# Attention scores of a hybrid encoder layer: 288 contraction rows packed as 128 + 128 + 32, and operands of the recurrence split by how long they live

## The chip, the cores and the metric

One core of one Trainium2 chip runs the whole layer in one launch. The metric is device time in microseconds (us). The engines named below are TensorE (PE, with its weight loads listed as PEld), VectorE (DVE), ScalarE (ACT), GpSimd (POOL) and SyncE (SP), which only issues transfers. TensorE's granted clock has two levels, 1.2 and 2.4 GHz; the profile gives it as a share of the higher one.

## The reference, cut to what matters

The layer normalises x (2048 positions, 1024 channels), projects it once, mixes positions in three branches (a Fourier transform, a gated delta-rule recurrence in both directions, attention with six heads), gates and projects each branch, merges them, and projects once more. The change touches attention and the recurrence:

```
s = einsum('bqhd,bkhd->bhqk', qn, k_nope) + einsum('bqhd,bkd->bhqk', qr, k_rope)   # 64 + 32 rows
p = softmax(s * 96 ** -0.5)
o = einsum('bhqk,bkhd->bqhd', p, v)
S = S * w + (S a) b^T + v k^T ;  y = S r         # per head (6), per direction (2), 2048 steps
```

`k_rope` is the same for all heads. All values are float32.

## The kernel before, in words

Products that need float32 accuracy are done in three passes: an operand is split in two parts, hi and lo, that TensorE multiplies in one pass each (type fp32r), and `mm3` (L140 to 144) adds hi*hi, hi*lo and lo*hi in one accumulator. Products of plain float32 operands (values, transposes, the recurrence) are given as they are; TensorE runs a float32 matmul as two instructions.

**Phase 1** (up to about 1408 us of the span) projects x. Its last part is `columns` (L359): three attention gates end it, two of them with their four position blocks in turn (L371). Beside it run `units` (L540), which builds the recurrence's operands per 64-position chunk and stores them in the scratch tensors `X_d` and `V_d`, and `inverses` (L736), a long chain of small VectorE operations on a tile `M` that is read from `X_d` and written back to it.

**Phase 2** (`phase2`, L1195, about 1408 to 2262 us) is attention over 24 windows: a head pair and 256 queries. A window has four units of 128 queries and one head, 96 units in all. For unit n, TensorE's order is written out by hand: four times [the scores of unit n+2 for one block of 512 keys (`scores`, three passes over 96 rows), four transposes of unit n's probabilities (`probs`)]; after the second and the fourth, some pieces of the values of the window before (`values`), and one `step` of a background list. VectorE moves each score block from PSUM to `S` and takes its maximum (L1307, "eviction" below), ScalarE does one exponential per unit (L1314), and the transposed blocks are copied to `PT`, two by ScalarE (L1033) and two by VectorE (L1032). Scores have three PSUM buffers, transposes two, values one.

The background list is, one after the other: the end of `units`, 12 waiting steps (`wait2`), `recurrence` (32 chunks of three steps: `seq_r` with the outputs `seq_y` of the chunk before, `seq_u`, `seq_s`; each step is 24 to 72 small TensorE instructions and two VectorE operations that the next step needs), `rwkv_out` (eight blocks of VectorE, ScalarE and GpSimd work on the recurrence's output), and `phase3_early` (weights of the last phase). The recurrence takes the two PSUM banks that are left. When it is over, `merged` is set and all value pieces come after the fourth block.

`seq_load` (L963) reads a chunk's operands: per direction one tile part of 8*64 columns from `X_d`, and two from `V_d`. `window_open` (L1254) requests a window's queries, `window_load` (L1267) a head pair's keys (two tiles with one buffer each), and, once, the values of all heads.

**Phase 3** does the projections and the output.

The framework fixes the order on every engine but TensorE in this stretch by priorities and its own estimate of times, and puts in the waits.

Of the kernel before, what the change touches and what calls it, by code (L numbers as in the profile page):

```python
# [90 lines left out]
class Trunk:  # L91
    def __init__(self, tc, ins, out, stop=99):
# [39 lines left out]
        self.wait2 = 12  # L132
# [145 lines left out]
    def scratch(self):  # L278
# [15 lines left out]
        self.qn_d = t([6 * 64, T // QB, 2 * QB], F32, name="qn_d")  # L294
        self.qr_d = t([6 * 32, T // QB, 2 * QB], F32, name="qr_d")
        self.kn_d = t([6 * 64, T // QB, 2 * QB], F32, name="kn_d")
        self.kr_d = t([32, T // QB, 2 * QB], F32, name="kr_d")
# [61 lines left out]
    def columns(self):  # L359
# [8 lines left out]
        gates = [(O_ZCG + n * P, self.to_gate(self.gc_d[n], self.nc.gpsimd)) for n in range(3)]  # L368
# [326 lines left out]
    def unit_x(self, it, up):  # L695
        nc, w, rev, V3 = self.nc, it["win"], it["rev"], self.V3
        X = it["X"] = up.tile([P, UC, 8, C], F32, tag="X", name=f'X{it["nm"]}', bufs=self.xb)
        for h in range(2):
            eng = nc.vector if h == 0 else nc.gpsimd
            ps = slice(64 * h, 64 * h + 64)  # L700
            eng.tensor_tensor(rev(X[ps, :, 2 * h, :]), V3(w["kk"][ps]), it["gexc"][ps], ALU.mult)
            eng.tensor_tensor(rev(X[ps, :, 2 * h + 1, :]), V3(w["r"][ps]), it["ginc"][ps], ALU.mult)

    def unit_gram(self, it, gps):
        nc, w, d, X, BK = self.nc, it["win"], it["d"], it["X"], it["BK"]
        p, u, nm = w["p"], w["u"], it["nm"]
        mk = lambda m, hv: m[hv].unsqueeze(1).to_broadcast([64, UC, P])
# [5 lines left out]
        for q in range(UC):  # L713
            for h, ps in enumerate((lo, up_)):
                nc.tensor.matmul(g[h][:, q, :], BK[ps, q, :], X[ps, q, 2 * h:2 * h + 2, :], start=True, stop=True)
        for h in range(2):
            kr, br = (up_, lo) if h == 0 else (lo, up_)
            nc.vector.tensor_tensor(X[br, :, 4:6, :].rearrange("p c s t -> p c (s t)"),
                                    g[h][br], mk(self.msk, br), ALU.mult)
            nc.vector.tensor_tensor(X[kr, :, 2 * h:2 * h + 2, :].rearrange("p c s t -> p c (s t)"),  # L720
                                    g[h][kr], mk(self.msr if d else self.msk, kr), ALU.mult)
        nc.scalar.activation(X[:, :, 6:8, :].rearrange("p c s t -> p c (s t)"), tp, AF.Copy)
# [5 lines left out]
    def unit_bonus(self, w, up, gps):  # L728
# [4 lines left out]
        nc.vector.tensor_tensor(bv, bp[:, :UN], w["v"], ALU.mult)  # L733
        nc.sync.dma_start(self.bv_d[p][:, w["sl"]], bv)

    def inverses(self, ip):  # L736
# [5 lines left out]
        def lanes(p, k):  # L742
            d, h, c = k // 4, k // 2 % 2, k % 2 * 16
            return (M[16 * k:16 * k + 16],
                    self.X_d[d][c:c + 16, :, p, 4 * C:5 * C].rearrange("c (h s) t -> c h s t", h=2)[:, h])
# [64 lines left out]
    def rope_tables(self, rp):  # L810
# [33 lines left out]
        for s in range(2):  # L844
            o = rp.tile([P, 2, W], F32R, tag="ko", name=f"ko{s}", bufs=2)
            self.split(o[:, 0, :], o[:, 1, :], z[:, 1, s, :], nc.gpsimd)
            nc.sync.dma_start(self.kr_d[16 * s:16 * s + 16].rearrange("f b t -> b f t"),
                              o.rearrange("p a t -> p (a t)").bitcast(F32))
# [14 lines left out]
    def mla_window(self, u, W, mp, mps, ones, wqh, wql, wkh, wkl):  # L863
# [28 lines left out]
        def emit(ps, M, dst):  # L892
# [3 lines left out]
            nc.sync.dma_start(dst, o[:M].rearrange("p a t -> p (a t)").bitcast(F32))  # L896

        for j in range(3):
# [3 lines left out]
            emit(ps[:, :W], P, self.kn_d[j * P:(j + 1) * P, u, :])  # L902
# [9 lines left out]
        for j in range(3):  # L912
# [4 lines left out]
            emit(ps[:, :W], P, self.qn_d[j * P:(j + 1) * P, u, :])  # L917
# [10 lines left out]
        qd = self.qr_d[:, u, :].rearrange("(h s f) t -> s h f t", s=2, f=16)  # L928
        for s in range(2):
            emit(t[:96, s, :], 96, qd[s])  # L930
# [3 lines left out]
    def recurrence(self):  # L934
        tc, nc = self.tc, self.nc
        with tc.tile_pool(name="sq", bufs=1, side="right", reuse_waits="tile") as sp, \
# [10 lines left out]
            yield  # L947
# [15 lines left out]
    def seq_load(self, sp, n):  # L963
        nc = self.nc
        X = sp.tile([P, 2, NP, 8, C], F32, tag="X", name=f"sX_{n}", bufs=2)
        W = sp.tile([P, 2, NP, 4, C], F32, tag="W", name=f"sW_{n}", bufs=3)
        for d in range(2):
            c = n if d == 0 else NCH - 1 - n
            nc.sync.dma_start(X[:, d].rearrange("p n s t -> p n (s t)"), self.X_d[d][c])
# [3 lines left out]
        return X, W  # L973
# [6 lines left out]
    def seq_r(self, ps, pad, n, cur):  # L980
        R, (X, W) = ps[0], cur
        for p in range(NP):
            for d, h, hs in self.lanes():
                self.nc.tensor.matmul(R[hs, d, p, :], X[:, d, p, 2 * h, :], W[:, d, p, 2 * h + 1, :], start=True, stop=True)
# [4 lines left out]
    def seq_u(self, ps, pad, n, cur):  # L989
        nc, U, (X, W) = self.nc, ps[1], cur  # L990
        for p in range(NP):
            for d, h, hs in self.lanes():
                nc.tensor.matmul(U[hs, d, p, :], X[:, d, p, 4, :], pad[0][h][:, d, p, :], start=True, stop=True)
# [503 lines left out]
```

## Time and profile before

| | us |
|---|---|
| median of three runs | 2632.16 (2631.91 to 2633.26) |
| the profiled execution | 2634.32 |
| its span, first to last instruction | 2632.5 |
| TensorE matmul busy | 2504.7 (95% of the span) |
| VectorE / ScalarE / GpSimd busy | 1737.4 / 991.9 / 848.0 |

Matmuls overlap their own tail with the next one, so a busy TensorE can still be given more; what one costs is the distance from its start to the start of the next. All numbers are from one execution.

### The profile page before, as it was taken

How to read it: one execution, taken by the hardware profiler on the slowest of the kernel's cores; microseconds unless marked ns; L12 is line 12 of the kernel's file. 1: busy time of each engine (PE TensorE's matmuls, PEld its weight loads, DVE VectorE, ACT ScalarE, POOL GpSimd, SP SyncE). 2: the span in 40 equal slices, each digit the busy share in tenths (PEclk: the TensorE clock that was granted, in tenths of full speed). 3: DMA queues.
4: the chain of work that ended last, by engine and by line, in shares of the span. 5: the costliest groups of instructions: out<-in, count | busy, mean ns of one | idle time of the engine just before them, and what ended most of it. 6: DMA issues, size and time to landing. Idle time of an engine off the chain costs nothing.

```text
span 2632.5 us, 46308 instructions
## 1 busy us (share of the span) xinstructions
PE 2504.7 (95%) x17295; PEld 2040.8 (78%) x17295; DVE 1737.4 (66%) x3432; ACT 991.9 (38%) x1929; POOL 848.0 (32%) x1124
## 2 busy tenths in 40 slices
PE   7989999999999999989998899999998899999998
PEld 6778887877777777768776688878876677799997
DVE  6236564388888859579398567766767787544444
ACT  6354443355555521111113333333355565322221
POOL 2244433355555511212220233323322220334342
PEclk9999999999999999999998899999999999999999
DMA  4353434477777774552733655665544311645452
GB/s 167 95 146 121 149 125 157 141 262 256 245 262 247 246 156 128 130 145 86 136 84 111 157 169 186 192 186 166 174 149 125 101 53 59 194 128 154 131 154 78
DMA packets 318443, 404.86 MB, mean 154 GB/s; under 512 B 56078, under 2 KB 225097, under 8 KB 317130
## 3 DMA queue, kind: packets, MB, share of 16 engines
q1 hardware_dynamic: 310762, 382.99, 49.0%
q0 software_dynamic: 7456, 18.91, 3.0%
q8 instruction: 137, 2.24, 0.4%
q14 instruction: 88, 0.72, 0.1%
HBM read 236.91 MB, written 164.89 MB: 153 GB/s over the span
## 4 chain that ended last, share of the span: by engine, by line
PE 38%; DVE 13%; DMA 8%; issue 4%; POOL 1%; ACT 1%; SPq 1%; DVEq 0%; POOLq 0%; ACTq 0%
PE av L1334 5%; PE tp L1322 4%; DVE M L760 4%; DVE tmp L758 4%; PE sc L142 3%; PE sc L144 2%; PE sc L143 2%; PE po L144 2%; PE po L143 2%; PE po L142 2%; PE p L144 2%; PE p L143 2%; PE p L142 2%; DVE S L1307 1%; PE mm L142 1%
## 5 line engine op out<-in xcount | busy, mean ns | idle before, releaser
L142 PE MATMUL mm<-hh,wh 128*128 128x512 f32 x1536 | 613.8, 400 | 6.5 <-ACT z L483 3.2
L144 PE MATMUL mm<-hh,wl 128*128 128x512 f32 x1536 | 604.0, 394 | 2.8 <-POOL wl L419 2.6
L143 PE MATMUL mm<-hl,wh 128*128 128x512 f32 x1536 | 605.2, 394 | 0.0
L142 PEld LDWEIGHTS mm<-hh,wh 128*128 128x128 f32 x1536 | 291.7, 190 | 72.1 <-ACT z L483 5.2
L144 PEld LDWEIGHTS mm<-hh,wl 128*128 128x128 f32 x1536 | 291.6, 190 | 65.1 <-POOL wl L419 4.1
L143 PEld LDWEIGHTS mm<-hl,wh 128*128 128x128 f32 x1536 | 291.9, 190 | 58.2 <-issue 1.0
L1307 DVE TENSOR_SCALAR_CACHE_REDUCE S<-sc 128x512 f32<-128x512 f32 x384 | 260.7, 688 | 73.2 <-PE sc L144 67.5
L419 POOL TENSOR_TENSOR wl<-wr,wh 128x256 fp32r<-128x256 f32 x192 | 172.2, 910 | 419.1 <-ACT wh L418 406.2
L1322 PEld LDWEIGHTS tp<-c_id,S 128*128 128x128 f32 x1536 | 192.9, 143 | 84.9 <-ACT PT L1033 14.5
L1322 PE MATMUL tp<-c_id,S 128*128 128x128 f32 x1536 | 237.8, 278 | 21.0 <-ACT S L1314 8.6
L1314 ACT ACTIVATE S<-S,m 128x2048 f32<-128x2048 f32 x96 | 192.2, 2003 | 161.7 <-DVE m L1312 161.7
L758 DVE TENSOR_TENSOR tmp<-M 128x62 f32<-128x62 f32 (+30 forms) x186 | 171.7, 923 | 96.5 <-DMA zm_d<-z 41.3
L142 PE MATMUL sc<-K,Q 96*128 96x512 f32 x384 | 188.4, 491 | 19.7 <-DVE S L1307 13.8
L1033 ACT ACTIVATE PT<-tp 128x512 f32<-128x512 f32 x192 | 113.2, 591 | 225.8 <-PE tp L1322 222.7
L1334 PE MATMUL av<-PT,V 128*64 128x256 f32 x1536 | 180.0, 385 | 0.0
L760 DVE TENSOR_TENSOR M<-M,tmp 128x62 f32<-128x62 f32 (+30 forms) x186 | 170.7, 918 | 5.8
L418 ACT ACTIVATE wh<-wr 128x256 fp32r<-128x256 f32 x192 | 74.4, 412 | 238.7 <-DMA wr<-in_w_in_dram 149.2
L144 PE MATMUL sc<-K,Q 96*128 96x512 f32 x384 | 155.4, 405 | 0.0
L143 PE MATMUL sc<-K,Q 96*128 96x512 f32 x384 | 154.8, 403 | 0.0
L483 ACT ACTIVATE z<-mm 128x512 f32<-128x512 f32 (+1 forms) x120 | 70.3, 589 | 217.7 <-PE mm L144 107.2
L1334 PEld LDWEIGHTS av<-PT,V 128*64 128x64 f32 x1536 | 105.4, 137 | 57.8 <-issue 11.2
L1432 POOL TENSOR_TENSOR g<-g 128x256 f32<-128x256 f32 x128 | 98.8, 774 | 143.2 <-DVE g L1430 100.6
(388 smaller groups left out, 4945.4 us busy)
## 6 DMA issues: line engine op xcount, KB each, us to landing
X_d<-X SPq DMA_DIRECT2D x96, 512.0 KB
sX<-X_d SPq DMA_DIRECT2D x64, 768.0 KB
wr<-in_w_in_dram SPq DMA_DIRECT2D x193, 128.0 KB
zm_d<-z SPq DMA_DIRECT2D x96, 256.0 KB
g<-zm_d SPq DMA_DIRECT2D x64, 384.0 KB
uu<-u_d SPq DMA_DIRECT2D x24, 512.0 KB
ul<-lo_d SPq DMA_DIRECT2D x48, 256.0 KB
sW<-V_d SPq DMA_DIRECT2D x128, 96.0 KB
```

What stands on the lines that cost most here:

```text
L142: mm(out, lh, rh, start=start, stop=False)
L143: mm(out, lh, rl, start=False, stop=False)
L144: mm(out, ll, rh, start=False, stop=stop)
L419: nc.gpsimd.tensor_tensor(wl[:, ks, :], wr, wh[:, ks, :].bitcast(F32), ALU.subtract)
L758: nc.vector.tensor_tensor(tv, M[:, 0:j, j:j + 1].to_broadcast([P, j, n]), M[:, j:j + 1, j + 1:C].to_broadcast([P, j, n]), ALU.mult)
L760: nc.vector.tensor_tensor(M[:, 0:j, j + 1:C], M[:, 0:j, j + 1:C], tv, ALU.add)
L1033: return self.nc.scalar.activation(out, src, AF.Copy)
L1307: nc.vector.tensor_scalar(u["S"][:, ks], sc, 1.0, -3.4e38, ALU.mult, ALU.max, accum_out=u["m4"][:, kb:kb + 1])
L1314: nc.scalar.activation(S, S, AF.Exp, scale=SM_SCALE, bias=m4[:, 5:6], accum_out=u["win"]["rs"][:, col:col + 1])
L1322: nc.tensor.transpose(tp[:, k, :], u["S"][:, (4 * g + k) * P:(4 * g + k + 1) * P], self.ident)
L1334: nc.tensor.matmul(av[64 * h:64 * h + 64, 0:QB], self.V[:, k, (2 * hp + h) * 64:(2 * hp + h + 1) * 64], PT[k // 4][:, k % 4, h, :], start= ...
L1432: nc.gpsimd.tensor_tensor(g, g, acc, ALU.add)
```

## The change

The scores' 3 * 96 = 288 contraction rows are laid out anew: pass one is [q_nope hi, q_nope hi] against [k_nope hi, k_nope lo], pass two [q_nope lo, q_rope hi, q_rope hi] against [k_nope hi, k_rope hi, k_rope lo], both over 128 rows; q_rope lo against k_rope hi is left, 32 rows. For it `KC` holds k_rope hi with one block of 512 keys in each quarter of the partitions, and `QC` q_rope lo four times; `scores_rest` does the four blocks of a unit with four matmuls, each on its own 32 rows and into its own accumulator, ahead of the unit's other scores. Score and transpose tiles now share one pool of five PSUM buffers. Scratch layouts keep hi and lo apart. Values are loaded per head pair.

The chunk operands `X_d` are reordered: 0 to 4 are what `seq_r`, `seq_u` and `seq_s` read, 5 to 7 what `seq_y` reads a step later; `seq_load` reads `V_d` first, then the two parts into tiles of their own. `wait2` goes from 12 to 9, and `recurrence` waits two steps more after its first load. `rwkv_out` requests its blocks two ahead and on ScalarE's queue, and its first addition moves from VectorE to GpSimd. One VectorE product in `unit_bonus` becomes a ScalarE copy and a GpSimd product. After the recurrence VectorE copies one `PT` block of four instead of two. Two gates of `columns` go through the position blocks in pairs, and their stores are issued by ScalarE instead of GpSimd. Weights of phase 3 are split one step after they are requested.

```diff
-        self.wait2 = 12
+        self.wait2 = 9
-        for tb in range(NTB):
+        for tbs in ((0, 1), (2, 3)):
             for w, consume in cols:
-                self.project(w, P, tb, consume, True)
+                for tb in tbs:
+                    self.project(w, P, tb, consume, True)
...
+            g4 = g[h].rearrange("p c (s t) -> p c s t", s=2)
+            nc.vector.tensor_tensor(X[br, :, 2:8:5, :], g4[br], mk(self.msk, br), ALU.mult)
+            nc.vector.tensor_tensor(X[kr, :, h:h + 6:5, :], g4[kr], mk(self.msr if d else self.msk, kr), ALU.mult)
...
-        nc.vector.tensor_tensor(bv, bp[:, :UN], w["v"], ALU.mult)
+        nc.scalar.activation(bv, bp[:, :UN], AF.Copy)
+        nc.gpsimd.tensor_tensor(bv, bv, w["v"], ALU.mult)
...
+        X = sp.tile([P, 2, NP, 5, C], F32, tag="X", name=f"sX_{n}", bufs=2)
+        Z = sp.tile([P, 2, NP, 3, C], F32, tag="Z", name=f"sZ_{n}", bufs=2)
...
+            nc.sync.dma_start(X[:, d].rearrange("p n s t -> p n (s t)"), self.X_d[d][c][:, :, 0:5 * C])
...
+            nc.sync.dma_start(Z[:, d].rearrange("p n s t -> p n (s t)"), self.X_d[d][c][:, :, 5 * C:8 * C])
...
-                    nc.sync.dma_start(t, src[:, :, sl].rearrange("n p t -> p n t"))
+                    nc.scalar.dma_start(t, src[:, :, sl].rearrange("n p t -> p n t"))
...
-                tc.tile_pool(name="scps", bufs=self.scb, space=PSUM, reuse_waits="tile") as scps, \
-                tc.tile_pool(name="tpps", bufs=self.tpb, space=PSUM, reuse_waits="tile") as tpps, \
+                tc.tile_pool(name="scps", bufs=5, space=PSUM, reuse_waits="tile") as scps, \
...
+                self.KC = ap.tile([P, TB], F32R, name="KC")
+                nc.sync.dma_start(self.KC.bitcast(F32), self.kr_d[0].rearrange("p (k t) -> k p t", t=TB))
...
+        for h in range(2):
+            qn, qr = [[src[a, (2 * hp + h) * n:(2 * hp + h + 1) * n, sl] for a in range(2)]
+                      for src, n in ((self.qn_d, 64), (self.qr_d, 32))]
+            for dst, src, n in ((qf[:, 0, h], qn[0], 64), (qf[0:64, 1, h], qn[1], 64), (qf[64:P, 1, h], qr[0], 32), (cf[:, h], qr[1], 32)):
+                nc.sync.dma_start(dst, src.unsqueeze(0).to_broadcast([dst.shape[0] // n, n, QB]))
...
+    def scores_rest(self, u):
+        qs = slice(u["q"] * P, (u["q"] + 1) * P)
+        u["sc"] = [self.scps.tile([P, TB], F32, tag="s", name=f'sc{u["nm"]}{kb}') for kb in range(NTB)]
+        for kb, sc in enumerate(u["sc"]):
+            ps = slice(32 * kb, 32 * kb + 32)
+            self.nc.tensor.matmul(sc, u["win"]["QC"][ps, u["h"], qs], self.KC[ps], start=True, stop=False)
...
-        self.mm3(sc, Q[:, 0, qs], Q[:, 1, qs], K[:, ws, 0, :], K[:, ws, 1, :], True, True)
+        for n in range(2):
+            nc.tensor.matmul(sc, Q[:, n, u["h"], qs], K[:, n, ks], start=False, stop=n == 1)
...
-        tp = self.tpps.tile([P, 4, P], F32, tag="tp", name=f'tp{u["nm"]}{g}')
+        tp = self.scps.tile([P, 4, P], F32, tag="s", name=f'tp{u["nm"]}{g}')
...
-        self.copy(g in self.ptd, dst, tp)
+        self.copy(g in (self.ptd[1:] if self.merged else self.ptd), dst, tp)
```

## Rows read from the trace of the kernel before

**Rows 1.** Busy us of each engine, clock and DMA by stretch: the recurrence, then after it.
```profile
1471.00:1940.00 469.00, 462.52 (x6048) 374.99 (x6049) 321.49 (x821) 171.85 (x258) 140.41 (x202) 0.99 0.57 171
1940.00:2262.00 322.00, 291.36 (x1974) 218.40 (x1974) 236.95 (x585) 180.97 (x248) 55.82 (x42) 0.97 0.34 97
```

**Rows 2.** Waits of TensorE, 1470 to 1940: waiter, awaited, us in total, times, longest.
```profile
PE sps L984 <- DMA sW<-V_d: 10.2, 2, 7.4
...
PE tp L1322 <- DVE PT L1032: 0.3, 1, 0.3
```

**Rows 3.** Waits of TensorE, 1940 to 2265.
```profile
PE sc L142 <- DVE S L1307: 13.8, 5, 6.5
PE tp L1322 <- ACT PT L1033: 6.7, 8, 2.8
...
PE tp L1322 <- DVE PT L1032: 4.4, 8, 2.7
```

**Rows 4.** Timeline during the recurrence: start, us, engine, line, instruction, count.
```profile
1700.81 0.40 PE L143 MATMUL sc<-K,Q 96*128 96x512 f32 x1
...
1701.04 0.40 PE L144 MATMUL sc<-K,Q 96*128 96x512 f32 x1
...
1701.28 0.60 PE L1322 MATMUL tp<-c_id,S 128*128 128x128 f32 x4
...
1701.81 0.92 PE L1006 MATMUL sps<-sW,sX 128*64 128x64 f32 x24
...
1702.66 0.50 PE L142 MATMUL sc<-K,Q 96*128 96x512 f32 x1
...
1703.00 0.39 PE L143 MATMUL sc<-K,Q 96*128 96x512 f32 x1
```

**Rows 5.** Timeline of TensorE in phase 1, around matmuls over 64 rows.
```profile
702.26 0.60 PE L711 MATMUL tp<-c_id,BK 128*128 128x128 f32 x4
702.79 1.16 PE L715 MATMUL g<-X,BK 64*128 64x128 f32 x16
```

**Rows 6.** Groups of the whole span: count | busy us, mean ns | idle before.
```profile
L715 PE MATMUL g<-X,BK 64*128 64x128 f32 x768 | 55.8, 285 | 0.0
...
L711 PE MATMUL tp<-c_id,BK 128*128 128x128 f32 x192 | 28.7, 272 | 0.0
```

**Rows 7.** The same groups, VectorE and ScalarE, 1940 to 2265.
```profile
L1307 DVE TENSOR_SCALAR_CACHE_REDUCE S<-sc 128x512 f32<-128x512 f32 x153 | 103.4, 685 | 14.3 <-PE sc L144 13.8
L1032 DVE COPY PT<-tp 128x512 f32<-128x512 f32 x81 | 55.6, 686 | 13.6 <-PE av L1334 11.0 <-PE tp L1322 2.6
L1307 DVE DVE_READ_ACCUMULATOR S<-sc 128x1 f32 x153 | 12.7, 83 | 0.0
...
L1062 DVE TENSOR_TENSOR ry<-ry,ry 128x768 f32<-128x768 f32 x8 | 8.6, 1074 | 21.7 <-issue 11.2 <-DMA ry<-y_d 10.5
```

**Rows 8.** The same groups, ScalarE, 1940 to 2265.
```profile
L1314 ACT ACTIVATE S<-S,m 128x2048 f32<-128x2048 f32 x39 | 78.0, 1999 | 32.0 <-DVE m L1312 32.0
L1033 ACT ACTIVATE PT<-tp 128x512 f32<-128x512 f32 x81 | 47.5, 589 | 66.6 <-PE tp L1322 63.6 <-PE av L1334 2.9
```

**Rows 9.** The same groups, VectorE, 1470 to 1940.
```profile
L1307 DVE TENSOR_SCALAR_CACHE_REDUCE S<-sc 128x512 f32<-128x512 f32 x195 | 132.8, 691 | 51.1 <-PE sc L144 46.1
...
L996 DVE COPY sW<-sps 64x384 f32<-64x384 f32 x64 | 35.5, 554 | 21.6 <-PE sps L993 17.2 <-DMA sX<-X_d 3.0
```

**Rows 10.** Timeline of SP's queue where the recurrence begins.
```profile
1466.71 1.18 SPq L971 DMA_DIRECT2D sW<-V_d  x2
```

**Rows 11.** Timeline of TensorE there; in brackets its idle time and what ended it.
```profile
1471.57 0.84 PE L984 MATMUL sps<-sW,sX 128*64 128x64 f32 x4 [7.39 <-DMA sW<-V_d]
1475.24 1.65 PE L984 MATMUL sps<-sW,sX 128*64 128x64 f32 x20 [2.83 <-DMA sW<-V_d]
```

**Rows 12.** One line of `unit_bonus`: ns least/median/most, first and last start.
```profile
L733 DVE TENSOR_TENSOR bv<-bp,uu x24: 405/408/416, 529.7 to 921.7; 128x256 f32<-128x256 f32 x24
```

**Rows 13.** The stores of `M` into `X_d`, in the same columns.
```profile
L766 POOL DMA_DIRECT2D X_d<-M x24: 763/763/842, 1091.6 to 1450.7; - x24
```

More of the change, by code (lines that the diff above doesn't have):

```diff
@@ L846, in rope_tables @@
             self.split(o[:, 0, :], o[:, 1, :], z[:, 1, s, :], nc.gpsimd)
-            nc.sync.dma_start(self.kr_d[16 * s:16 * s + 16].rearrange("f b t -> b f t"),
-                              o.rearrange("p a t -> p (a t)").bitcast(F32))
+            for a in range(2):
+                nc.sync.dma_start(self.kr_d[a, 16 * s:16 * s + 16].rearrange("f (b t) -> b f t", t=W), o[:, a, :].bitcast(F32))
         yield
@@ L895, in emit @@
             nc.vector.scalar_tensor_tensor(o[:M, 1, :], ps, 1.0, o[:M, 0, :].bitcast(F32), ALU.mult, ALU.subtract)
-            nc.sync.dma_start(dst, o[:M].rearrange("p a t -> p (a t)").bitcast(F32))
+            for a in range(2):
+                nc.sync.dma_start(dst(a), o[:M, a, :].bitcast(F32))
         for j in range(3):
@@ L946, in recurrence @@
             nc.gpsimd.memset(cur[1][64:P, :, :, 3, :], 0.0)
-            yield
+            for _ in range(3):
+                yield
             for n in range(NCH):
@@ L972, in seq_load @@
                                   self.V_d[c * C:(c + 1) * C, :, h, :])
-        return X, W
+        for d in range(2):
+            c = n if d == 0 else NCH - 1 - n
+            nc.sync.dma_start(X[:, d].rearrange("p n s t -> p n (s t)"), self.X_d[d][c][:, :, 0:5 * C])
+        for d in range(2):
+            c = n if d == 0 else NCH - 1 - n
+            nc.sync.dma_start(Z[:, d].rearrange("p n s t -> p n (s t)"), self.X_d[d][c][:, :, 5 * C:8 * C])
+        return X, W, Z
     HALF = (slice(0, 64), slice(64, P))
@@ L980, in seq_r @@
     def seq_r(self, ps, pad, n, cur):
-        R, (X, W) = ps[0], cur
+        R, (X, W, _) = ps[0], cur
         for p in range(NP):
             for d, h, hs in self.lanes():
-                self.nc.tensor.matmul(R[hs, d, p, :], X[:, d, p, 2 * h, :], W[:, d, p, 2 * h + 1, :], start=True, stop=True)
+                self.nc.tensor.matmul(R[hs, d, p, :], X[:, d, p, h, :], W[:, d, p, 2 * h + 1, :], start=True, stop=True)
         with self.after(-self.first):
@@ L989, in seq_u @@
     def seq_u(self, ps, pad, n, cur):
-        nc, U, (X, W) = self.nc, ps[1], cur
+        nc, U, (X, W, _) = self.nc, ps[1], cur
         for p in range(NP):
             for d, h, hs in self.lanes():
-                nc.tensor.matmul(U[hs, d, p, :], X[:, d, p, 4, :], pad[0][h][:, d, p, :], start=True, stop=True)
+                nc.tensor.matmul(U[hs, d, p, :], X[:, d, p, 2, :], pad[0][h][:, d, p, :], start=True, stop=True)
         with self.after(-self.first):
@@ L1005, in seq_s @@
             for d, h, hs in self.lanes():
-                nc.tensor.matmul(S[hs, d, p, :], X[:, d, p, 6 + h, :], W[:, d, p, 2 * h, :], start=True, stop=True)
+                nc.tensor.matmul(S[hs, d, p, :], X[:, d, p, 3 + h, :], W[:, d, p, 2 * h, :], start=True, stop=True)
         with self.after(-self.first):
@@ L1066, in rwkv_out @@
                 yield
+                yield
+                if b + 2 < T // W:
+                    tiles.append(load(b + 2))
                 mu = rps.tile([P, 4, W], F32, tag="mu", name=f"mu{b}")
@@ L1079, in rwkv_out @@
                 self.blocksums(var, hi, lo)
+                if b + 1 < T // W:
+                    nc.gpsimd.tensor_tensor(tiles[b + 1][0], tiles[b + 1][0], tiles[b + 1][1], ALU.add)
                 va = rp.tile([P, NP, W], F32, tag="rva", name=f"rva{b}", bufs=1)
@@ L1210, in phase2 @@
                     units.append(self.unit_load(n))
+                self.scores_rest(units[n])
                 for kb in range(NTB):
@@ L1219, in phase2 @@
                         units.append(self.unit_load(n + self.la))
+                        self.scores_rest(units[-1])
                     for g in range(4):
@@ L1350, in values, with phase3_weights @@
         return [lambda j=j: piece(j) for j in range(nk // 2)] + [finish]
-    def phase3_weights(self, k, wp, rp, bufs):
+    def phase3_weights(self, k, wp, rp, bufs, wait=True):
         nc = self.nc
@@ L1368, in phase3_weights @@
             lo = wp.tile([P, D], F32R, name=f"w3l{k}")
+        if wait:
+            yield
         for n in range(2):
@@ L1381, in phase3_early @@
             for k in range(self.early):
-                self.phase3_weights(k, wp, rp, 1)
-                yield
+                yield from self.phase3_weights(k, wp, rp, 1)
             while not self.y0_ready:
@@ L1413, in phase3 @@
             for k in range(8, 16):
-                self.phase3_weights(k, wp, self.hk, 2)
+                for _ in self.phase3_weights(k, wp, self.hk, 2, False):
+                    pass
             for b in range(T // W):
```

98 lines of the change are left out of this document (45 added, 53 removed).

## The prediction

> **What bounds the kernel now.** First the busy times of all engines by stretch, to see who is the bound where the change acts: during the recurrence TensorE has 462.5 of 469 us under a matmul, VectorE 321; after it TensorE 291 of 322, VectorE 237, ScalarE 181 [rows 1]. Then TensorE's waits, which say whether anything else ever holds it. During the recurrence next to nothing does: 10.2 us for the first `V_d` loads, 0.3 for transposes [rows 2]. After it 13.8 us go to score accumulators that VectorE has not emptied, and 6.7 and 4.4 to transposes whose buffers ScalarE and VectorE have not copied [rows 3]. So in the first stretch a TensorE instruction less is time less, and in the second mostly. Last the timeline of one slot, for the true price of an instruction: a score pass starts 0.23 us after the pass before it (1700.81, 1701.04), not the 0.40 that its own length shows, and four transposes take the rest of a slot [rows 4].
>
> **The third pass and what replaces it.** A unit gives up one pass in each of its four blocks: 4 x 0.23 = 0.92 us. It gets four matmuls over 32 rows and 512 columns. What those cost hangs on whether matmuls on different rows run side by side. The trace has such a case with two halves: 16 matmuls over 64 rows last 1.16 us from the first start to the last end [rows 5]; less the 0.285 of one [rows 6], 15 starts take 0.88 us. Transposes, with as many columns per instruction, start (0.60 - 0.27)/3 = 0.11 us apart [rows 5, 6]; one by one the 16 would need 15 x 0.11 = 1.65. So two halves do overlap. No row shows four quarters: the ends are one pass for all four, 0.23, and four in a row, 0.92. I take 0.23, as the halves lose little.
>
> Beside this there is a cost of going into and out of such a group. Transposes end their run at 1701.28 + 0.33 and the next would start at 1701.72; the recurrence's small matmuls start at 1701.81 instead: 0.09. After them the first score pass starts at 1702.66 and the second at 1703.00: 0.34 in place of 0.23, as its weights were not loaded ahead: 0.11 [rows 4]. A rest group behind a recurrence step or values thus adds 0.09 + 0.11 + 0.23 = 0.43, as the way out was paid before; net -0.49 a unit. Behind transposes it pays the way out as well: 24 small matmuls occupy 0.85 us from their start to the next pass, of which (0.92 less a tail estimated at 0.2) 0.72 are theirs, so 0.13, and 0.11 again [rows 4]; some 0.67 in all, net -0.25. After the recurrence about half of the units end in values: on average -0.37.
>
> By evictions, 195/4 = 49 units fall into the recurrence [rows 9] and 153/4 = 38 behind it [rows 7]: 49 x 0.49 = 24 us and 38 x 0.37 = 14 us less.
>
> The Trainium skill (TensorE: Matmul & The Clock Gate, Measured speedup vs the span model) gives four such row tiles of 512 columns a speedup of 3.07, not 4. By that the group would take 0.92/3.07 = 0.30 instead of 0.23, and all 87 units 6 us more; the halves above, 1.65/0.88 = 1.9 of 2, agree as far as they go. Against the change speaks another page (TensorEngine Tiling (Array Packing), Key Properties): a change of the tiling mode drains the engine. The 0.09 above is what this trace shows for it, 8 us over 87 groups; they are in the sum already.
>
> **Five PSUM buffers for scores and transposes.** `scores_rest` takes four at once, so that the first transposes of the next unit need the last buffer of the old one copied, and the second need the first eviction done. Behind a waiting transpose stand all scores and steps, since TensorE's order is fixed. How tight this is: outside the value pieces a unit costs VectorE four evictions (0.69 + 0.08), two copies (0.69) and, in the recurrence, 2 x 2 operations of 0.55: 3.1 + 1.4 + 2.2 = 6.7 us and its small reductions [rows 7, 9]. TensorE will need four slots of 0.92 (two passes, four transposes at 0.11), the rest group 0.43 and two steps of about 1.1: 6.3. VectorE then is no faster than TensorE in the units without values, some five in eight. The wait is not shown by any row: it is at least -11 us (the transposes' waits of rows 3 vanish) and at most one copy, 0.69, for each of 87 units, 60 us. I take 0.25 a unit in the recurrence, where transposes now wait 0.3 us in all, and 0.15 behind it: 12 + 6 = 18 us. There ScalarE takes three copies of four: 2.0 + 3 x 0.59 = 3.8 us a unit [rows 8], and VectorE drops to 3.8; both below the slots' 4.1.
>
> **`rwkv_out`.** VectorE stood 21.7 us before its first addition (L1062), 10.5 of it for the transfer [rows 7], and TensorE's 13.8 us behind evictions [rows 3] come from such stands in VectorE's queue. Requested two blocks ahead and added on GpSimd, which is busy 56 of 322 us [rows 1], that goes: I take -10 of 13.8; ends 0 and -14. The 32 requests come onto ScalarE's queue; at SP's 0.59 each [rows 10] they are 19 us beside 181 busy of 322, hidden; if one waits for its buffer, an exponential waits behind it. That is in the 6 us above.
>
> **The start of the recurrence.** TensorE stands 7.4 + 2.8 us there for `V_d` [rows 11]. But these loads are issued at 1466.7 [rows 10], and the last store of `M` is issued at 1450.7 [rows 13]: what comes late is the inverse, which the change leaves on VectorE. With `V_d` first the loads overlap better (-3); what the first six units save is waited out; and the first step comes one half unit sooner (9 + 3 waits in place of 12 + 1), so half a unit of scores less is done by then, up to 4 us later. Together +1, ends -6 and +6.
>
> **Edits at nothing.** The product of `unit_bonus` is 24 x 0.41 = 10 us off VectorE [rows 12], which is not the bound in phase 1; ScalarE and GpSimd have room for as much; 0, at the ends -3 and +3. The reordered `X_d` keeps the number of instructions and the bytes; its loads become shorter runs, two transfers more per chunk, 2 x 0.59 of SP's time in about 14 us. Queries take eight transfers instead of two: 24 x 6 x 0.59 = 85 us of SP's queue over some 780 us, with `V_d` and `X_d` loads queued behind; requested half a window early, hidden. If not, a chunk is late by a few of them, 2 us, at up to 32 chunks: this is the upper end. The pairs of gates and their queue: 0.
>
> **Sum.** -24 - 14 + 18 - 10 + 1 = -29 us. On the profiled execution's 2634.3 (span 2632.5 and 1.8 around it) that is 2605; the median of the runs lies 2.2 lower, so the median forecast is 2603.
>
> **Rivals.**
> 1. *The buffers do not bind.* The whole saving shows, and VectorE's relief with it: without the 18, and with the 14: -24 - 14 - 14 + 1 = -51, 2581. For it: VectorE is idle for 148 of 469 us [rows 1]. Against: that idleness lies in the value pieces.
> 2. *VectorE takes over as the bound of the recurrence.* Nothing is gained there, as its 6.7 us and the reductions replace TensorE's; behind it -10 and a little: 2620 to 2632, I say 2628.
> 3. *Slower: transposes wait behind the exponential.* The first transposes of a unit need a buffer that ScalarE copies after its 2.0 us exponential. If the copies fall behind it, each unit waits about 2.0 + 0.59 less the 1.6 of two slots: 1.0 us. It decides once the wait passes 0.55 a unit. 87 x 1.0 in place of the 18: -29 - 18 + 87 = +40, 2672. For it: 6.7 us of waits for ScalarE's copies already [rows 3]. Against: in the recurrence there are none.
> 4. *The quarters run one by one* (the change does not do what it says): 87 x 0.69 = 60 more, of which the 18 of waits fall away as TensorE is slower: +13, 2645. Against: the halves of rows 5.
>
> **Chances.** Forecast 0.48, rival 1 0.24, rival 2 0.12, rival 3 0.09, rival 4 0.07. A measurement of this kernel tells 0.2%, 5 us, from no change. Faster: all of the forecast but a tail of 0.03, rival 1, a third of rival 2: 0.73. Same: two thirds of rival 2 and part of the tail: 0.10. Slower: rivals 3 and 4 and the rest: 0.17. The range goes from a little below rival 1, where all low ends meet, to rival 4: 2565 to 2645; outside are rival 3 and a tenth.
>
> **What would show it.** Right: four rest matmuls with starts a few ns apart and under 0.7 us from the last instruction of a unit to its first score pass; slots of 0.92 us; the recurrence stretch some 12 us shorter, the one behind it some 18; L1062's stand gone. Wrong: starts of the four 0.23 us apart (rival 4); TensorE waiting in L1322 or the rest for VectorE (rival 2) or ScalarE (rival 3) by over 50 us in all. The prediction fails as a whole if the recurrence starts later than 1480 us or the median leaves the range.

## The result: slower by 0.9%, and the profile after

The changed kernel takes 2654.43 us (median of four runs, 2646.05 to 2661.13) beside 2632.08 for the kernel before in the same session: ratio 1.0087, 95% interval 1.0069 to 1.0105. The forecast was 2603, its range 2565 to 2645. The profiled execution after is the fastest of the four, 2646.05 (span 2644.3), so the traces explain 12 of the 22 us between the medians. What made the other runs longer is in no trace and stays open; the two longest, 2658 and 2661 us, had a mean granted clock of 0.975 and 0.974, the other two 0.981.

Where the 12 us lie (starts and ends of groups of instructions in both traces):

| | before | after | |
|---|---|---|---|
| last product of `units` (L715, now L716) | 924.0 | 937.9 | +13.9 |
| first score | 1407.6 | 1433.0 | +25.4 |
| first matmul of the recurrence | 1471.6 | 1484.9 | +13.3 |
| the recurrence | 464.2 | 462.1 | -2.1 |
| from there to the last values | 327.4 | 325.4 | -2.0 |
| the rest, to the end of the span | 369.3 | 371.9 | +2.6 |

The two stretches of [rows 1], after, in the same columns (span, then busy us of PE, PEld, DVE, ACT, POOL, clock, DMA share, GB/s):
```profile
1485.00:1947.00 462.00, 441.56 (x6024) 338.89 (x6024) 318.66 (x819) 171.98 (x257) 139.29 (x200) 0.99 0.68 186
1947.00:2272.00 325.00, 295.26 (x2025) 208.25 (x2022) 214.73 (x550) 205.35 (x297) 73.44 (x52) 0.96 0.38 110
```
TensorE is 21 us less under a matmul in the recurrence, yet the stretch is only 2 us shorter: TensorE, the engine that bounds it, now stands. Its waits there, for [rows 2] (waiter, awaited, us in total, times, longest):
```profile
PE tp L1349 <- DVE S L1334: 8.0, 24, 0.5
PE sps L993 <- DMA Q<-qn_d: 6.4, 1, 6.4
PE sps L993 <- POOL sW L1021: 4.6, 11, 0.6
PE sps L993 <- DMA sX<-X_d: 0.9, 1, 0.9
```
and behind it, for [rows 3]:
```profile
PE tp L1349 <- ACT PT L1042: 9.4, 6, 7.3
PE tp L1349 <- DVE S L1334: 5.7, 7, 3.3
PE sc L1325 <- ACT PT L1042: 5.6, 5, 2.6
PE var L177 <- POOL rlov L809: 3.3, 1, 3.3
PE mu L177 <- POOL rlom L809: 2.5, 1, 2.5
```
A slot of the timeline, for [rows 4]:
```profile
1706.77 0.92 PE L1015 MATMUL sps<-sW,sX 128*64 128x64 f32 x24
1707.62 0.51 PE L1325 MATMUL sc<-KC,QC 32*128 32x512 f32 x4
1708.06 0.73 PE L1333 MATMUL sc<-K,Q 128*128 128x512 f32 x2
1708.62 0.60 PE L1349 MATMUL tp<-c_id,S 128*128 128x128 f32 x4
1708.98 0.71 PE L1333 MATMUL sc<-K,Q 128*128 128x512 f32 x2
```
The four rest matmuls start within 10 ns and the next pass 0.44 us after them; a slot is 1708.98 - 1708.06 = 0.92. That is what was forecast. To tell work from waiting I sum the distances from each start on TensorE to the next by kind and neighbours; the shortest of each kind, times its count, is the work, what lies above it the waiting (us; groups cut by the edges are left out). Waiting is put to the group at whose start the distance begins: in the recurrence "scores+rest" is nearly all transposes that could not start behind the scores, and 6.4 of the 9.9 us under "transposes" are a step behind them that waited for the operands of one chunk.
```
                          work   waiting: scores+rest  transposes  recurrence's steps  its sums
recurrence, before       449.3             3.7            1.3           4.8
recurrence, after        424.5            15.4            9.9          11.3
behind it, before        275.1            23.5           18.4                            1.2
behind it, after         260.5            42.4            6.6                            7.7
behind it, e4            284.3            26.5            4.3                            7.0
```
(e4 holds 72 value instructions that the cut took from the others, 7.8 us.)

Two more rows. Ahead of the first score (start, us, instruction, in brackets the idle time and what ended it), TensorE had ended its last column at 1411:
```profile
1433.03 0.80 PE L1325 MATMUL sc<-KC,QC 32*128 32x512 f32 x4 [21.97 <-DMA QC<-qr_d]
```
And in `units`, the largest wait of ScalarE and one wait of TensorE, before, after, and in g1 (told below); TensorE waits there 17.7 us in all before, 28.1 after and 13.9 in g1:
```profile
ACT vt L631 <- DMA bv_d<-bv: 49.5, 18, 4.1
PE bp L731 <- DVE kds L682: 12.3, 9, 2.0
```
```profile
ACT vt L632 <- DMA bv_d<-bv: 71.1, 23, 5.4
PE wps L649 <- ACT X L722: 16.3, 7, 3.5
```
```profile
ACT z L484 <- PE mm L144: 39.6, 17, 2.4
PE wps L649 <- ACT X L722: 4.7, 6, 1.5
```

### The profile page after: what moved, and what is told of

The parts are those of the page before. It is cut to its first block, busy times and chain, and to the rows that moved or that the text cites. A ratio compares the mean times of both kernels' runs of the same rounds, so it can differ in the third digit from the quotient of the medians.

```text
span 2644.3 us, 46656 instructions
## 1 busy us (share of the span) xinstructions
PE 2480.1 (94%) x17295; PEld 1985.4 (75%) x17295; DVE 1712.6 (65%) x3359; ACT 1021.7 (39%) x1994; POOL 879.7 (33%) x1144
## 5 line engine op out<-in xcount | busy, mean ns | idle before, releaser
L1333 PE MATMUL sc<-K,Q 128*128 128x512 f32 x768 | 279.5, 446 | 0.0
L1349 PEld LDWEIGHTS tp<-c_id,S 128*128 128x128 f32 x1536 | 184.4, 142 | 105.8 <-DVE S L1334 51.8
L1042 ACT ACTIVATE PT<-tp 128x512 f32<-128x512 f32 x233 | 134.6, 591 | 187.2 <-PE tp L1349 172.0
L1333 PEld LDWEIGHTS sc<-K,Q 128*128 128x128 f32 x768 | 118.3, 194 | 29.0 <-issue 25.1
L1041 DVE COPY PT<-tp 128x512 f32<-128x512 f32 x151 | 103.8, 688 | 18.9 <-PE av L1364 15.0
```

Source lines behind the costliest of these rows:

```text
L1042: return self.nc.scalar.activation(out, src, AF.Copy)
L1333: nc.tensor.matmul(sc, Q[:, n, u["h"], qs], K[:, n, ks], start=False, stop=n == 1)
L1349: nc.tensor.transpose(tp[:, k, :], u["S"][:, (4 * g + k) * P:(4 * g + k + 1) * P], self.ident)
```

## The experiments

Ratios are to the kernel before, each with its 95% interval. Runs of one letter share a session. "Grams" are the products of L715 (L716), the last of `units`.

### The product of `unit_bonus`: e1, e2, f2, g1

e1 is the changed kernel with this one edit undone, e2 the kernel before with this edit alone:
```diff
-        nc.scalar.activation(bv, bp[:, :UN], AF.Copy)
-        nc.gpsimd.tensor_tensor(bv, bv, w["v"], ALU.mult)
+        nc.vector.tensor_tensor(bv, bp[:, :UN], w["v"], ALU.mult)
```


> The changed kernel with one edit undone: the product of unit_bonus is one VectorE operation again. Theory A (this edit makes the delay of phase 1: ScalarE's copy into the buffer that a store still reads makes ScalarE, and behind it TensorE, wait): the last gram matmul (L715 or its line) goes back from 937 to about 923 us, the first step of the recurrence from 1485 to about 1472, and the whole from 2654 to about 2640. Rival B (the strided halves of the tile X, or the products moved between engines, make it): the end of the grams stays near 937 and the time near 2654.

> The kernel before with this one edit made (the product of unit_bonus as a ScalarE copy and a GpSimd product). Theory A: grams end near 937 instead of 923, the recurrence starts some 13 us later, 2645 in all. Rival B: 2632, no change.

e1: 1.0022 (1.0009 to 1.0035), grams to 924.3, recurrence from 1475.0. e2: 1.0045 (1.0029 to 1.0061), grams to 936.7, recurrence from 1484.4. That is theory A in both: the edit costs 13 us of phase 1 with or without the rest of the change, and 12 to 17 us of the whole. But e1 is still no faster than the kernel before, so this edit isn't the whole loss. f2 asks by which wait, ScalarE's copy into the buffer:
```diff
-        nc.scalar.activation(bv, bp[:, :UN], AF.Copy)
-        nc.gpsimd.tensor_tensor(bv, bv, w["v"], ALU.mult)
+        nc.scalar.activation(w["kds"], bp[:, :UN], AF.Copy)
+        nc.gpsimd.tensor_tensor(bv, w["kds"], w["v"], ALU.mult)
```


> The changed kernel, but ScalarE's copy of unit_bonus goes into the tile kds, whose content is no longer needed, and only the GpSimd product writes the tile bv, which shares its buffer with vt. Theory A (ScalarE, which works in order, waits in this copy for the store of the buffer's former content, and the operands of the next units behind it): the grams end near 923 again, the whole near 2640. Rival B (GpSimd's additional work delays its other products, kds first): grams still end near 937, 2654.

1.0086 (1.0066 to 1.0107), grams to 942.3, rival B's time: my first reason was wrong. It is not the copy that waits but the next `vt`, which has the buffer (tag "vt") after `bv` and is written by ScalarE too (77.5 us of that wait in f2, 71.1 in the changed kernel). g1 takes `bv` out of that buffer and leaves both engines as changed:
```diff
-        bv = up.tile([P, UN], F32, tag="vt", name=f"bv{p}{u}")
+        bv = w["kds"]
```


> The changed kernel, unit_bonus with both operations as changed (ScalarE copy, GpSimd product), but in place in the tile kds, from which it is stored; the buffer that bv and vt shared then belongs to vt alone. Theory A (what the edit costs is that the store of bv starts later, behind two more queues, and that ScalarE's copy into vt waits for that store: 71 us in 23 waits after, 49.5 in 18 before): that wait vanishes, the grams end at 924 or earlier, the whole 2640 or less. Rival B (GpSimd itself, 20 us busier in this stretch, delays kds and the products behind it): grams end near 937, 2654.

0.9990 (0.9976 to 1.0004), grams to 913.0. The wait of 71.1 us is gone from ScalarE's list (its row of g1 above shows what leads it now), and `units` ends even 11 us ahead of the kernel before, whose 49.5 us in that wait were not free either. GpSimd's added work costs nothing that shows (h1, below, with the product on VectorE and in `kds`: grams to 911.1).

### With the scores' part alone, without it, and without the split by life: e3, e4, h3

> The kernel before with the scores' part alone: the new layouts in scratch, 128 + 128 + 32 rows, five shared PSUM buffers, values per head pair. Theory A (the repacking gives some 38 us gross, and loses it in two places: waits for PSUM buffers of over 20 us, and a late first score, since KC and QC come last in SP's queue): recurrence stretch 455 to 465 us instead of 465, the first score some 20 us after the last column, the whole 2615 to 2640. Rival B (the repacking by itself loses): slower than 2640. Rival C (it gains its 25 to 30 and the other edits lose them): 2600 to 2610.

> The changed kernel with the scores' part undone (layouts, packing, buffers, values as in the kernel before); all other edits stay. Theory A: the other edits lose some 14 us in phase 1 by the product of unit_bonus and win little behind the recurrence: 2635 to 2650. Rival C (the other edits lose more than the scores' part gains): 2665 or more. If the requests of rwkv_out gain their 10 us, some 2635.

e3: 1.0369 (1.0336 to 1.0401), 2727 us: rival B, and 87 us beyond the 2640 that it names. e4: 1.0027 (1.0014 to 1.0041), 2637 us, theory A. Behind the recurrence e4's TensorE no longer waits for VectorE's evictions, but more than before for ScalarE, which now takes three copies of four:
```profile
PE tp L1334 <- ACT PT L1041: 16.8, 22, 2.0
```
In e3 TensorE stands in the recurrence for
```profile
PE sps L985 <- DMA sX<-X_d: 59.5, 19, 8.3
```
The kernel before, with the same single load per chunk, had none of it, beside keys of 3.1 MB in place of 4.2 and two requests for queries in place of eight. h3 is the changed kernel with that load put back, which means `X_d` in the old order, as one part, and requested ahead of `V_d`:
```diff
-            nc.sync.dma_start(X[:, d]..., self.X_d[d][c][:, :, 0:5 * C])
-            nc.sync.dma_start(Z[:, d]..., self.X_d[d][c][:, :, 5 * C:8 * C])
+            nc.sync.dma_start(X[:, d]..., self.X_d[d][c])
```


> The changed kernel with the chunk operands as before: X_d in the old order and loaded as one part, ahead of V_d. Theory A (the split by life is what lets the operands come in time beside the larger loads of keys and queries; e3_only_scores, which had the packing without it, waited 59.5 us for sX): TensorE waits some 50 us for sX, 2700 or more. Rival B (the waits of e3_only_scores came from another edit that it lacked, such as the two steps of wait after the first load): 2654 to 2665.

1.0315 (1.0293 to 1.0337), theory A, and the same wait:
```profile
PE sps L988 <- DMA sX<-X_d: 54.6, 18, 16.8
```
So the split, which the prediction had among the edits at nothing, is worth 2.3% as soon as the scores are packed. How much of this is the shorter life of a buffer, and how much the order of the requests, wasn't tried apart.

### Requests: f1 and g2

f1 (on e1) asks for a window's queries in four transfers, for which the scratch of the queries holds the heads side by side:
```diff
-        self.qn_d = t([2, 6 * 64, T], F32, name="qn_d")
+        self.qn_d = t([2, 64, T // QB, 6, QB], F32, name="qn_d")
...
+            nc.sync.dma_start(dst.rearrange("p h t -> p (h t)"), src.unsqueeze(0).to_broadcast([dst.shape[0] // n, n, 2 * QB]))
```


> The changed kernel with the product of unit_bonus on VectorE (as e1_no_bonus, the comparison for the next three runs), and a window's queries requested by four transfers in place of eight: the scratch of the queries keeps the two heads side by side, same bytes, runs twice as long. Theory A (the number of requests in SP's one queue is what delays the first score by 22 us, the operands of one chunk by 6.4 us and a weight of the last phase by 7.4 us): these three shrink by half or more, the recurrence starts 5 to 10 us sooner, and the whole comes from 2635 to about 2620. Rival B (the bytes make it: the keys are 4.2 MB per head pair in place of 3.1): no change, 2635.

1.0376 (1.0358 to 1.0394): its phase 1 came out in another order (the grams begin at 603.6 us, not at 523.1), so the total says nothing. From the first score to the end of the span it takes 1217.0 us, e1 1214.2, and the waits for QC (26.2 us, e1 22.3) and for a chunk's operands (15.6 us, e1 6.7) have not shrunk. Halving the requests took nothing off them.

g2 (on e1) moves KC and the first QC to ScalarE's queue:
```diff
-                nc.sync.dma_start(self.KC.bitcast(F32), ...)
+                nc.scalar.dma_start(self.KC.bitcast(F32), ...)
```


> As e1_no_bonus, but KC and the first window's QC are requested on ScalarE's queue instead of behind the keys and two windows of queries on SP's. Theory A (TensorE's 22 us of idle time before the first score is the place of these two in SP's in-order queue): the first score starts near 1400 to 1405 in place of 1419, the recurrence, which starts when TensorE comes to it, some 10 us earlier, the whole 2623 to 2628. Rival B (their memory, part of the last phase's, or the transfers of 4.2 MB of keys, are what is late): first score still near 1419, 2635.

1.0051 (1.0036 to 1.0066); first score at 1421.7, no earlier (e1 1419.1): rival B's time. ScalarE's timeline shows why: KC goes out right behind the last store of a gate, and the gates are late, each waiting for the store of an earlier one:
```profile
1405.55 0.60 ACT L473 ACTIVATE zg<-mm 128x512 f32<-128x512 f32 x1 [10.00 <-DMA gc_d<-zg]
...
1410.47 0.60 ACT L473 ACTIVATE zg<-mm 128x512 f32<-128x512 f32 x1 [4.32 <-DMA gc_d<-zg]
1412.22 0.33 ACTq L475 DMA_DIRECT2D gc_d<-zg  x1
1412.59 1.11 ACTq L1219 DMA_DIRECT2D KC<-kr_d  x1
```
From this request to the first score it is 9.1 us. The first scores of the kernel before read nothing that is loaded so late. That KC also waits for the memory of phase 1 was only argued.

### Buffers: f3, f4, i1

f3 (on e1) leaves q_rope lo times k_rope hi out, and each accumulator is taken where its two passes begin:
```diff
-            self.nc.tensor.matmul(sc, u["win"]["QC"][ps, u["h"], qs], self.KC[ps], start=True, stop=False)
```


> As e1_no_bonus, but the product of q_rope lo and k_rope hi is left out: no rest matmuls, and each score accumulator is taken only where its two passes begin; all transfers stay. Theory A (holding four of five PSUM buffers from the start of a unit is what costs, some 20 us of waits in the recurrence and some 15 behind it): beside the 0.44 us of 84 units, 37 us, the waits for buffers fall too, together 55 to 70 us less, 2565 to 2580. Rival B (the waits are VectorE's and ScalarE's pace, not the early hold): only the matmuls' time goes, at most 37 us, 2600 or more, and the time of the transposes stays near 0.58 us a slot.

1.0005 (0.9994 to 1.0016), 2629 us: within rival B's "2600 or more", but for a reason that neither theory had. With no reader left for QC, SP requested the QC of all 24 windows at once, 48 transfers ahead of the first chunk, and TensorE stood:
```profile
PE sps L992 <- DMA sX<-X_d: 62.9, 5, 53.4
```
Behind that stand the theory can be read: the two passes between transposes take 0.554 us on average (after: 0.695, shortest 0.544), so the early hold of four buffers does cause these waits; and the recurrence and the stretch behind it are 24 and 35 us shorter than in e1, 59 in all and so within the 55 to 70 of theory A, of which the expectation gives 37 to the matmuls left out. But the steps of the recurrence then wait more (8.8 us for GpSimd, e1 4.6).

f4 (on e1) only reorders TensorE, so that a transpose takes over a score buffer one slot later:
```diff
                     for g in range(4):
-                        if nxt:
-                            self.scores(units[-1], g)
+                        for kb in ((0,), (1, 2), (3,), ())[g]:
+                            if nxt:
+                                self.scores(units[-1], kb)
                         self.probs(units[0], g)
```


> As e1_no_bonus, with another order on TensorE: the scores of block 3 of 4 (in the order 0, 1, 2, 3: block 2) come ahead of the second transposes and the last block ahead of the third, so that a transpose that takes the buffer of a score block comes one slot later after that block's passes. Nothing else changes. Theory A (in the recurrence transposes wait 0.2 to 0.6 us, 24 times and more, because the buffer that they take over is still being moved by VectorE): the waits 'tp for S' of 7.5 us and the slots above 0.55 us vanish, 10 to 15 us less in the recurrence. Rival B (VectorE's queue, not the distance, sets it, and evictions now come in a bunch): no change or longer.

0.9983 (0.9966 to 0.9999), 10 us under e1; the 7.5 us of "tp for S" are gone in the recurrence, which is 5 us shorter, not the 10 to 15 of theory A, and what is late next is seen:
```profile
PE sps L992 <- DMA sX<-X_d: 10.6, 2, 9.7
PE sps L992 <- POOL sW L1020: 10.3, 20, 0.6
```
i1 (on h2, below) changes who copies behind the recurrence:
```diff
-        self.copy(g in (self.ptd[1:] if self.merged else self.ptd), dst, tp)
+        self.copy(g in ((2, 3) if self.merged else self.ptd), dst, tp)
```


> As h2_keys_kept_late_weights, but once the recurrence is over VectorE copies the third and fourth transposed block of a unit (the changed kernel: the fourth alone), ScalarE the first two. The rest matmuls of a unit take over the buffer of the third block of the unit before. Theory A (behind the recurrence the rest matmuls wait for ScalarE's copy, which stands behind its 2.0 us exponential, the third rival of the prediction): the waits 'sc for PT of ScalarE', 8.8 us, fall to under 3, the stretch behind the recurrence becomes 5 to 10 us shorter. Rival B (VectorE's queue then makes the same wait): no difference.

0.9828 (0.9809 to 0.9847) beside 0.9882 for h2, and the stretch 302.2 us instead of 321.3: theory A, and twice what it said. The sum of distances gives 18 of these 19 us to the waiting of scores and rest, 39.5 us in h2 and 21.2 in i1. i1 both gives VectorE a second copy and picks other blocks for it; how much each does wasn't tried apart. Rows of h2, then of i1:
```profile
PE sc L1326 <- ACT PT L1041: 8.8, 6, 2.4
PE tp L1350 <- DVE S L1335: 7.9, 4, 4.7
```
```profile
PE tp L1350 <- DVE S L1335: 3.8, 3, 3.0
PE tp L1350 <- DVE PT L1040: 2.3, 4, 1.5
PE sc L1326 <- ACT PT L1041: 1.8, 1, 1.8
```

### Mending the packed kernel: g3, h1, h2, i2, and without packing g4, h4

g3 is f4 with the product on VectorE and in place in `kds`, and three requests on other queues (KC and the first QC as in g2, the keys of later head pairs through `kq`, and early weights):
```diff
+            kq = nc.scalar if k else nc.sync
...
-        nc.sync.dma_start(raw, src)
+        (nc.gpsimd if wait else nc.sync).dma_start(raw, src)
```


> The changed kernel with five edits together: the product of unit_bonus on VectorE and in place in kds; the order of f4_order; KC and the first QC on ScalarE's queue as in g2; the keys of the second and third head pair on ScalarE's queue, so that the operands of a chunk don't stand behind 4.2 MB; the early weights of the last phase on GpSimd's queue. Theory A (the loss of the change is in waits around transfers and buffers, the packed scores themselves give some 43 us): 2595 to 2612. Rival B (the waits move elsewhere, the recurrence's own chain of steps and the evictions hold TensorE): 2618 to 2626, no better than f4_order.

0.9940 (0.9922 to 0.9957), 2612 us, the upper end of theory A: the sum of f4 and the `kds` edit, nothing for the queues. The stand for a chunk's operands became one for ScalarE, which waits for the keys' buffer in order:
```profile
PE sps L1001 <- ACT ys L1035: 8.6, 1, 8.6
PE tp L1350 <- ACT PT L1041: 4.1, 1, 4.1
```


> As e4_all_but_scores (all edits but the scores' repacking), with the product of unit_bonus on VectorE and in place in kds. Theory A (of the other edits only that of unit_bonus loses, and the wait of vt for the store of bv costs also in the kernel before): grams end before 920, and the whole is some 15 us below e4_all_but_scores, near 2620. Rival B (that wait is hidden before): as e4 less the price of the edit, some 2625.

0.9929 (0.9902 to 0.9956), grams to 911.4, theory A: with this mending alone, the kernel without the packing is as fast as the one with it.

h1 (f4 with `kds`, all requests on SP) keeps the key tiles, and the k_rope rows in them:
```diff
+                kt = self.win[k - 1]["K"][h] if k else self.hk.tile(...)
...
+                if k == 0:
+                    nc.sync.dma_start(kf[64:P, 1], self.kr_d...)
```


> The changed kernel with the product of unit_bonus on VectorE and in place in kds, the order of f4_order, and the tiles of the keys kept over the head pairs, so that the k_rope rows, which are the same for all heads, are loaded once: 3.1 MB per later head pair in place of 4.2, as in the kernel before. All requests stay on SP's queue. Theory A (the wait of the recurrence for a chunk at the change of the head pair, 9.7 us in f4_order, comes from the bytes that the packing added): that wait is under 3 us, the recurrence stretch near 448 us, the whole 2600 to 2606. Rival B (the place of the requests in the queue makes it, whatever their bytes): wait still 8 to 10 us, 2610 to 2614.

0.9898 (0.9875 to 0.9921); the longest wait for sX is 7.2 us, not 9.7. By its time, 2601 us, it is theory A; by the wait it lies between the two: a quarter of the keys' bytes less took a quarter of it away. This is one wait in one trace (with the same keys it is 3.6 us in h2, 4.5 in i1, 6.5 in i2), so what share the bytes have stays open. h2 adds the last phase's early loads on GpSimd's queue, with two steps between request and use; h4 is g4 with the same:
```diff
+                    self.nc.gpsimd.dma_start(yr[n], self.ys_d[k + n][:, 0:256])
+                yield
+                yield
```


> As h1_keys_kept, with the early weights of the last phase and its first inputs requested on GpSimd's queue, the inputs two at a time with two steps between request and use. Theory A (the 6 to 7 us for which TensorE stands near 2180 us are ScalarE waiting, in order, for such an input): that stand is gone, 5 to 8 us less than h1_keys_kept. Rival B (what is late next takes its place): no difference.

> As g4_no_repack_kds (all edits but the scores' repacking, the product of unit_bonus in place in kds), with the last phase's early loads as in h2. It is the comparison for h2: Theory A (once its waits are gone, the packing pays): h2 is faster than this by 5 to 15 us. Rival B (what the packing gives back in waits for buffers, for the first KC and QC and in the recurrence's own chain is all that it gains): equal or this one faster, 2600 to 2608.

h2: 0.9882 (0.9852 to 0.9912), not to be told from h1: the longest wait for ScalarE's copy behind the recurrence falls from 5.2 to 2.4 us, but their sum only from 9.9 to 8.8, and the stretch is no shorter (321.3 us, h1 318.0): rival B. h4: 0.9895 (0.9864 to 0.9926). h2 and h4 can't be told apart either, though the work of h2, by the sum of distances, is 37 us less in the two stretches: rival B.

i2 is i1 with `seq_y` ahead of `seq_r`:
```diff
+                if n:
+                    self.seq_y(ps, pad, n - 1, prev)
                 self.seq_r(ps, pad, n, cur)
-                if n:
-                    self.seq_y(ps, pad, n - 1, prev)
```


> As i1_copies_2_3, and in each chunk of the recurrence the 48 matmuls of seq_y, whose operands are long there, go ahead of the 24 of seq_r, which wait for GpSimd's product. Theory A (with the packed scores the recurrence's own chain, step by step, is late by 0.5 to 0.8 us in 20 of 32 chunks, 10.3 us in all): these waits vanish, the recurrence stretch becomes some 10 us shorter, 2580 to 2588. Rival B (seq_r then ends 1.4 us later and VectorE's copy of it, so that the step behind it waits): same length.

0.9794 (0.9770 to 0.9819), 2575.22 us, the fastest kernel of this study. "sps for POOL sW" is no longer in the list and the recurrence takes 446.3 us in place of 451.7; half of the expected 10 came. Its two stretches:
```profile
1458.00:1905.00 447.00, 436.24 (x6030) 344.03 (x6029) 313.58 (x821) 170.19 (x257) 138.23 (x200) 0.98 0.71 191
1905.00:2207.00 302.00, 287.30 (x2023) 209.44 (x2023) 235.92 (x589) 183.50 (x256) 81.88 (x68) 0.98 0.38 115
```
VectorE is 21 us busier behind the recurrence than in the changed kernel and TensorE 23 us sooner done. Whether i1's and i2's edits would also help a kernel without the packing was not tried, so what the packing is worth in the end isn't shown.

## Why the prediction was wrong, by its steps

The profiled execution was forecast at 2605 us and took 2646: 41 us, of which 12 lie in the start of the recurrence (forecast +1, measured +13.3), 10 in the recurrence (-12 and -2.1), 16 behind it (-18 and -2.0) and 3 in the rest. So more than one step failed. The first below that did was a term put at nothing without a look at its buffer; the largest were the waits behind the recurrence.

- **The scores' matmuls, -24 and -14.** Right: 449.3 to 424.5 and 275.1 to 260.5 us of work, -24.8 and -14.6. The rest group cost 0.44, forecast 0.43. By the Trainium skill's 3.07 (TensorE: Matmul & The Clock Gate, Measured speedup vs the span model) it would be, as an estimate, 0.09 + 0.11 + 0.30 = 0.50; the trace is nearer to the full overlap.
- **`unit_bonus`, "0, at the ends -3 and +3": the first step that failed.** The busy times of three engines were weighed and the tag of the buffer was not. e1 and e2 show that it costs 13 us of phase 1, g1 that the shared buffer is the reason. The same wait is in the trace before, 49.5 us of ScalarE.
- **The start of the recurrence, +1, ends -6 and +6.** It was +13.3, past the point of 1480 at which the prediction said it would fail. With `unit_bonus` undone it is 1475.0 (e1), and in g1 1464.4, so some 10 of the 13 us came from that edit (alone, in e2, it makes 12.8). It came by two ways side by side: the last store of `M` is issued at 1458.2 in place of 1450.7 (e1: 1448.4), and TensorE's last column ends at 1411 in place of 1402 (e1: 1397). From 1390 to 1490 TensorE waits for no operand of the recurrence in the changed kernel, so there its own order came last, with the 22 us before the first score in it. That score, 25 us later than before, was not foreseen. Its wait is not mended in any kernel here (i2 still has 22.2 us), and what it costs by itself is not shown.
- **The five buffers in the recurrence, +12.** Right in size: the waiting that the table has under scores and rest rose by 11.7 us, and f4 shows its cause.
- **The recurrence's own chain, not in the sum.** The waiting of its steps rose from 4.8 to 11.3 us: among it are waits for GpSimd's product, on which the next step hangs (1.5 us before, in a row that [rows 2] leaves out, 4.6 after, 10.3 in f4). i2 takes 5 us out by putting `seq_y` ahead.
- **Behind the recurrence, +6 for buffers and -10 for `rwkv_out`: the step that failed by most.** In e4, without the packing, waiting of scores and transposes falls from 41.9 to 30.8 us, 11 for the 10 forecast, but 5.8 came back in the sums (`mu`, `var`), which now wait for GpSimd. The 13.8 us behind VectorE's evictions are gone there, but the waits for ScalarE's copies rose from 6.7 to 16.8. With the packing the waiting of scores, rest and transposes is 49.0, so the buffers cost up to 18, not 6; 7.3 of them are one wait for a copy behind which ScalarE stood for a weight of the last phase. Late copies on ScalarE, the mechanism of the third rival, decide here, and only here, though not at its 87 us; i1 takes 19 us out of this stretch. That it is the exponential ahead of a copy, and not one copy too many on ScalarE, is only argued. I had put the engines' busy times beside the slots and not asked when a copy that stands behind 2.0 us of exponential is needed.
- **Eight transfers for the queries, 0.** One chunk waits 6.4 us in the recurrence, at the change of the head pair. f1 speaks against the number of requests, h1 gives the keys' bytes a part; the rest is open.
- **The reordered `X_d`, 0.** In the changed kernel it costs nothing that shows (0.9 us of waits for sX), and the packing needs it (h3: 2.3%). As "nothing" it was right only by luck.
- **Rivals 1, 2 and 4** did not come: buffers bound, VectorE was no longer busy than before, the quarters ran side by side. The recurrence gained as little as rival 2 said, but by other waits.

## What to carry to other kernels

When an operation is moved to another engine, look first at the tile it writes: who has the buffer before and after it, and which in-order engine waits for its store. When work goes off the bound engine, list the waits that its length used to cover, with the buffer, the copy and the step each belongs to: here 39 us less of matmuls left the packed kernel level with the unpacked one (h2, h4), and another order of transposes, another engine for a copy and another order of two steps took some 10, 19 and 5 us of such waits away. And an edit that is put at nothing (the split of `X_d`) may be what another one needs; undo it alone before calling it nothing.

## What was not expected of the hardware

- A request itself can be long: among f3's requests of queries on SP's queue, one lasted 11.4 us, the others from 0.49 us. Columns: least, median and most ns, first and last start.
```profile
L1280 SPq DMA_DIRECT2D Q<-qn_d x4: 687/2934/11379, 1453.8 to 1470.1; - x4
L1280 SPq DMA_DIRECT2D Q<-qr_d x2: 493/1202/1912, 1467.4 to 1473.8; - x2
```
- The 22 us without a matmul ahead of the first score are seen in TensorE's granted clock: 0.79 from 1410 to 1420 us, 0.50 (1.2 GHz) from 1420 to 1430, and 0.69 in the ten us in which scores begin again.
